# Feed-forward parts of a two-block network on one core: the fourth and fifth chunk sums in the banks of Strassen's products, the root's spread behind block 70

## The chip, the core and the metric

The kernel runs on one core of a Trainium2 chip. The metric is the device time of one execution in microseconds (us). A core has five engines that run their own instruction streams side by side: PE (TensorE: matrix products; its weight loads are listed apart as PEld), DVE (VectorE), ACT (ScalarE), POOL (GpSimd) and SP (SyncE, which issues the transfers here). PSUM is the memory into which PE accumulates; this kernel uses it as eight banks, in three pools.

## The reference, cut to what matters

Two layers over 256 tokens of width 2048. Each layer has a mixer (a convolution and pooling mixer in the first layer, a short gated convolution in the second) and a feed-forward part, each added to the residual stream `h`:

```
h = h + mixer(h)
h = h + swiglu(rms_norm(h, ffn_norm[i]), w_gate[i], w_up[i], w_down[i])
# swiglu(h, g, u, d) = (silu(h @ g) * (h @ u)) @ d,   g, u: 2048 x 5632,   d: 5632 x 2048
# rms_norm: h * rsqrt(mean(h*h over the 2048) + 1e-6) * gain
```

The root of a token's mean square is one number per token. It is not multiplied into `h`: the matrix products run on `h * gain`, and the root is multiplied into their results afterwards. So the products can begin before the root is known; only what leaves PSUM needs it.

## The kernel before, in words

**Precision.** All is single precision in and out. Each 128x128 block of weights is split into a rounded part `hi` (ACT, line 200) and the remainder `lo` (DVE, line 201), and so are the activations (`xs`: ACT line 316, DVE line 317). A block then takes three matmuls over 256 tokens, `product`, lines 290 to 292. "Block" below means those three. Weights come in tiles of 16 blocks and are split eight blocks at a time, some pieces ahead; the split pieces lie in five buffers for `hi` and five for `lo`.

**Chunk sums.** In a feed-forward part 16 blocks make one chunk sum: 128 columns of the gate or of the up matrix over the whole width. Gate and up take turns. A chunk sum lies in a PSUM bank of the pool `acc`, which has three banks, until DVE has multiplied it by the root (`scaled`, line 444). A second pool, `s`, has four banks for the second way in which a part of the columns is computed: Strassen's seven products (`s_stream`, lines 746 to 748), which begin later and need token-major sums of `h` (`s_forms`, lines 662 to 669, ACT and DVE, eight pieces). The last PSUM bank, `st`, holds small sums.

**The root.** After the last residual chunk: square (ACT, line 421), sum over chunks (POOL, line 423), sum over the partitions by PE (line 359), root on ACT (line 372), a few operations on 128x2 numbers on DVE (lines 373 to 380), a diagonal matrix (DVE, line 384), a matmul of it with ones that spreads the root over all partitions (PE, line 392), a copy to SBUF (DVE, line 430). Then the first chunk sums can be evicted. In the source all of this is called after the first chunk sum of the part, and the eight pieces of `s_forms` are queued there, one every six blocks.

**What sets the order.** A table, `KINDS`, says for each step whether a block of the column products or a step of Strassen's products comes next; `LEAD` (line 60) says how many blocks precede the first Strassen step of the first window of a feed-forward part, and runs of 14 steps are then dealt out evenly. On top of it a scheduler that simulates a timeline sets each engine's own order when the program is built, so an instruction can stand earlier or later on its engine than in the source. On the chip each engine works through its own order.

**Names.** FFN0 and FFN1 are the feed-forward parts of the two layers. Blocks are counted from 0 at the start of such a part: chunk sum 1 is blocks 0 to 15, chunk sum 4 blocks 48 to 63, chunk sum 5 blocks 64 to 79.

## Time and profile before

| | |
|---|---|
| median of 3 runs | 2024.15 us (2020.88 to 2025.91) |
| the profiled execution, its own time | 2023.4 us |
| its span, first to last instruction | 2021.4 us |
| mean granted TensorE clock | 0.994 |
| PE busy | 1991.6 us (99%) |
| DVE busy | 1693.5 us (84%) |
| ACT busy | 1145.3 us (57%) |
| POOL busy | 197.6 us (10%) |

The profile is of one execution. Its span leaves out 2.0 us around the first and the last instruction that the time holds. A busy share is a mean over stages with different limits; a stall of some microseconds shows in a stage's own rows only. In the timeline a row gives the start, the duration, the engine, the source line, the operation, its output and inputs, and in brackets how long the engine sat idle ahead of it and what ended that. Matmul rows overlap: each shows some 0.28 us, while the next begins 0.11 us after it. In the view of engine windows each stretch has, for each engine, its busy time and in brackets the count of instructions, and then the granted clock and the share of the DMA engines.

### The profile page before, as it was taken

The page shows a single profiled execution, that of the slowest core. Times are in us where ns is not written, and L with a number is a line of the kernel's source. Part 1 is how long each engine was busy: PE and PEld are TensorE (multiplying, and loading weights), DVE is VectorE, ACT ScalarE, POOL GpSimd, SP SyncE. Part 2 cuts the span into 40 slices and gives each one's busy share as a digit, 9 for nine tenths or more (in the row PEclk, how much of TensorE's full clock was granted, in tenths as well). Part 3 has the DMA queues.
Part 4 walks back from the last instruction along what each step waited for, and adds up shares of the span by engine and source line. Part 5 has one row for each costly group of instructions (what it writes and reads, how often), then busy time and mean ns, then how long its engine had stood idle before and what let it go on. Part 6 is the DMA issues. An engine that isn't in the chain of part 4 may idle for free.

```text
span 2021.4 us, 41502 instructions
## 1 busy us (share of the span) xinstructions
PE 1991.6 (99%) x17370; PEld 1987.4 (98%) x17370; DVE 1693.5 (84%) x2370; ACT 1145.3 (57%) x1492; POOL 197.6 (10%) x180
## 2 busy tenths in 40 slices
PE   9999899999999999999999999999999999999998
PEld 8999899999999999999999999999999999999998
DVE  6998878988898888998666666778888898899995
ACT  7786665555555555556444444655555555555555
POOL 2996200000000000002000001100000000000003
PEclk9999999999999999999999999999999999999999
DMA  8555345555556555555555555455555464545562
GB/s 332 187 185 191 134 150 215 200 191 206 197 200 216 201 208 190 205 195 220 194 189 190 200 195 189 167 188 208 188 196 219 171 224 180 221 177 200 209 231 83
DMA packets 56923, 396.16 MB, mean 196 GB/s; under 512 B 6432, under 2 KB 7200, under 8 KB 9760
## 3 DMA queue, kind: packets, MB, share of 16 engines
q1 hardware_dynamic: 56736, 393.52, 52.7%
q8 instruction: 136, 2.23, 0.4%
q14 instruction: 51, 0.42, 0.1%
HBM read 391.39 MB, written 2.10 MB: 195 GB/s over the span
## 4 chain that ended last, share of the span: by engine, by line
PE 92%; DVE 5%; ACT 1%; DMA 1%; issue 0%; SPq 0%; DVEq 0%; ACTq 0%
PE acc L290 23%; PE acc L291 23%; PE acc L292 23%; PE s L748 7%; PE s L746 7%; PE s L747 7%; DVE side L514 1%; DVE side L516 1%; DVE lo L201 1%; PE acc L702 0%; ACT hi L200 0%; DMA rows<-in_xtok 0%; DMA h<-in_xT 0%; ACT w L662 0%; DVE sf L669 0%
## 5 line engine op out<-in xcount | busy, mean ns | idle before, releaser
L200 ACT CAST hi<-w 128x1024 fp32r<-128x1024 f32 (+2 forms) x916 | 915.3, 1009 | 787.8 <-PE acc L291 481.1
L201 DVE TENSOR_TENSOR lo<-w,hi 128x1024 fp32r<-128x1024 f32 (+2 forms) x867 | 1004.6, 1174 | 214.4 <-ACT hi L200 199.0
L290 PE MATMUL acc<-xs,hi 128*128 128x256 f32 x2688 | 743.5, 277 | 6.8 <-DVE gate L444 3.5
L291 PE MATMUL acc<-xs,hi 128*128 128x256 f32 x2688 | 742.1, 277 | 0.0
L292 PE MATMUL acc<-xs,lo 128*128 128x256 f32 x2688 | 738.9, 277 | 0.1
L290 PEld LDWEIGHTS acc<-xs,hi 128*128 128x128 f32 x2688 | 507.7, 189 | 8.6 <-ACT hi L200 3.3
L291 PEld LDWEIGHTS acc<-xs,hi 128*128 128x128 f32 x2688 | 507.7, 189 | 0.0
L292 PEld LDWEIGHTS acc<-xs,lo 128*128 128x128 f32 x2688 | 505.4, 189 | 0.6 <-DVE lo L201 0.5
L290 PE MATMUL acc<-y,hi 128*128 128x256 f32 x1408 | 388.5, 276 | 0.0
L291 PE MATMUL acc<-y,hi 128*128 128x256 f32 x1408 | 387.6, 276 | 0.0
L292 PE MATMUL acc<-y,lo 128*128 128x256 f32 x1408 | 385.5, 276 | 0.0
L291 PEld LDWEIGHTS acc<-y,hi 128*128 128x128 f32 x1408 | 264.4, 188 | 0.0
L290 PEld LDWEIGHTS acc<-y,hi 128*128 128x128 f32 x1408 | 264.2, 188 | 0.0
L292 PEld LDWEIGHTS acc<-y,lo 128*128 128x128 f32 x1408 | 263.3, 188 | 0.0
L423 POOL TENSOR_TENSOR sumsq<-sumsq,sq 128x256 f32<-128x256 f32 x56 | 55.7, 995 | 1540.6 <-ACT sq L421 1540.4
L746 PE MATMUL s<-hi,sf 128*128 128x256 f32 x704 | 193.7, 276 | 0.0
L747 PE MATMUL s<-hi,sf 128*128 128x256 f32 x704 | 193.3, 276 | 0.0
L748 PE MATMUL s<-lo,sf 128*128 128x256 f32 x704 | 191.7, 276 | 0.0
L747 PE MATMUL s<-hi,xs 128*128 128x256 f32 x528 | 146.1, 277 | 0.0
L748 PE MATMUL s<-lo,xs 128*128 128x256 f32 x528 | 145.9, 276 | 0.0
L746 PE MATMUL s<-hi,xs 128*128 128x256 f32 x528 | 145.7, 276 | 0.0
L747 PEld LDWEIGHTS s<-hi,sf 128*128 128x128 f32 x704 | 132.2, 188 | 0.0
(162 smaller groups left out, 2386.3 us busy)
## 6 DMA issues: line engine op xcount, KB each, us to landing
w<-in_wall SPq DMA_DIRECT2D x365, 1024.0 KB, 4.9
w<-in_wall SPq DMA_DIRECT2D x7, 512.0 KB, 8.3
rows<-in_xtok SPq DMA_DIRECT2D x2, 1024.0 KB, 7.8
h<-in_xT SPq DMA_DIRECT2D x7, 256.0 KB, 7.3
out<-res SPq DMA_DIRECT2D x2, 512.0 KB, 2.7
out<-res SPq DMA_DIRECT2D x2, 384.0 KB, 2.8
v<-in_vec SPq DMA_DIRECT2D x1, 260.0 KB, 6.7
h<-in_xT SPq DMA_DIRECT2D x2, 128.0 KB, 2.4
```

The lines of the kernel that those rows point to most:

```text
L200: nc.scalar.copy(hi, src)
L201: engine.tensor_tensor(out=lo, in0=src, in1=hi, op=ALU.subtract)
L290: nc.tensor.matmul(acc, hi, x[:, :T], start=first, stop=False)
L291: nc.tensor.matmul(acc, hi, x[:, T:], start=False, stop=False)
L292: nc.tensor.matmul(acc, lo, x[:, :T], start=False, stop=last)
L423: nc.gpsimd.tensor_tensor(out=self.sums[0], in0=self.sums[0], in1=sq, op=ALU.add)
L514: nc.vector.scalar_tensor_tensor(out=dst, in0=src, scalar=wt, in1=dst, op0=ALU.mult, op1=ALU.add)
L516: nc.vector.tensor_tensor(out=side, in0=side, in1=prods.pop((c, k)), op=ALU.add)
L746: nc.tensor.matmul(acc, xh, hi, start=first, stop=False, skip_group_check=True)
L747: nc.tensor.matmul(acc, xl, hi, start=False, stop=False, skip_group_check=True)
L748: nc.tensor.matmul(acc, xh, lo, start=False, stop=last, skip_group_check=True)
```

## The change

In the first window of each feed-forward part:

- `LEAD` goes from 76 to 96. By the table the first run of Strassen's steps moves from behind 113 blocks to behind 128, and the four runs then stand 32 blocks apart in place of 37; the last one stays behind block 224.
- The fourth and fifth chunk sums go into the first two banks of the pool `s`, which Strassen's products use later.
- The work on the root is cut in two. The first part (sums, root, diagonal) is called after the first chunk sum as before. The second part (the spreading matmul and the copy) is called at 70 blocks, and the scheduler is told to put that matmul behind the last matmul issued so far. Evictions of chunk sums that end before are held back and done right then.
- The eight pieces of `s_forms` are queued from 28 blocks on in place of 16.

Nothing is computed that was not computed before, and nothing is left out.

```diff
-LEAD = (76,) + (0,) * len(SECTIONS)
+LEAD = (96,) + (0,) * len(SECTIONS)
+FORMS_AT, REST_AT = 28, 70
...
-        nc.tensor.matmul(acc, lo, x[:, :T], start=False, stop=last)
+        state_pe["last"] = nc.tensor.matmul(acc, lo, x[:, :T], start=False, stop=last).ins
...
-        return spread or over_features(diag)
+        if halves:
+            return spread
+        return partial(over_features, diag)
...
-        def rstd(self, sums=None, keep=None):
-            st = rsqrt_of(*self.sums, scale=1.0 / D, st=sums, keep=keep)
-            r = tmp.tile([P, T], F32, name="rstd", bufs=1)
-            nc.vector.tensor_copy(out=r, in_=st)
-            return r
+        def rstd(self, sums=None, keep=None, behind=False):
+            spread = rsqrt_of(*self.sums, scale=1.0 / D, st=sums, keep=keep)
+
+            def rest():
+                with tc.issue_after(state_pe["last"]) if behind else nullcontext():
+                    st = spread()
+                r = tmp.tile([P, T], F32, name="rstd", bufs=1)
+                nc.vector.tensor_copy(out=r, in_=st)
+                return r
+
+            return rest if behind else rest()
...
             def rstd():
-                state["r"] = norm.rstd(keep=rtok)
+                state["rest"] = norm.rstd(keep=rtok, behind=True)
+
+            def token_sums():
                 scratch = wst.tile([P, 16 * P], F32, name="w")
...
+                            if w == 0 and jobs in (3, 4):
+                                acc = banks["s"].tile([P, 2 * T], F32, name=f"s{jobs - 3}")[:, :T]
+                            else:
+                                acc = new_acc()
...
+                                at = cursor["P"] - first_block
+                                if w == 0 and at == FORMS_AT:
+                                    token_sums()
+                                if w == 0 and at == REST_AT:
+                                    state["r"] = state["rest"]()
+                                    while held:
+                                        held.pop(0)()
+                            jobs += 1
+                            if w == 0 and jobs == 1:
+                                rstd()
+                            evict = partial(up_of, pair, c, acc) if half else partial(gate_of, pair, acc)
+                            if "r" in state:
+                                evict()
                             else:
+                                held.append(evict)
```

Line numbers shift in the changed kernel: there 291 to 293 are the three matmuls of a block, 202 is `lo`, 361 the sum over partitions, 386 the diagonal, 396 the spreading matmul, 438 the copy, 454 the multiplication by the root.

**First place: PE around the spread in FFN0.** `acc_3547` is the third chunk sum, `acc_3633` the fourth, `s1_3685` the fifth in the changed kernel; the numbers are tiles. Before:

```order
L290 MATMUL acc_3547<-xs_75,hi_3468 128x256
L291 MATMUL acc_3547<-xs_75,hi_3468 128x256
L292 MATMUL acc_3547<-xs_75,lo_3469 128x256
L392 MATMUL st_3459<-diag_3456,ones_76 128x256
L290 MATMUL acc_3633<-xs_75,hi_3504 128x256
L291 MATMUL acc_3633<-xs_75,hi_3504 128x256
L292 MATMUL acc_3633<-xs_75,lo_3505 128x256
```

The change:

```order
L292 MATMUL s0_3602<-xs_75,hi_3520 128x256
L293 MATMUL s0_3602<-xs_75,lo_3521 128x256
L291 MATMUL s1_3685<-xs_75,hi_3564 128x256
...
L293 MATMUL s1_3685<-xs_75,lo_3565 128x256
L396 MATMUL st_3716<-diag_3456,ones_76 128x256
L291 MATMUL s1_3685<-xs_75,hi_3564 128x256
```

Before, the spread stands between block 47 and block 48; in the change it stands behind block 69, inside the fifth chunk sum. In FFN1 it stands at the same places.

**Second place: DVE around the copy of the root in FFN0.** `lo_...` are split weights for blocks 72 and 80 (before) and 80, 88, 96 and 104 (change), `sf` are the last pieces of `s_forms`. Before:

```order
L201 TENSOR_TENSOR lo_3635<-w_3508,hi_3634 128x1024
L669 TENSOR_TENSOR sf_3384<-w_3463,sf_3384 128x512
L380 COPY rtok_3385<-st_3441 128x2
L384 TENSOR_TENSOR diag_3456<-v_73,st_3441 128x128 x2
L201 TENSOR_TENSOR lo_3671<-w_3596,hi_3670 128x1024
L430 COPY rstd_3461<-st_3459 128x256
L444 TENSOR_TENSOR gate_3464<-acc_3386,rstd_3461 128x256
L444 TENSOR_TENSOR val_3542<-acc_3467,rstd_3461 128x256
L444 TENSOR_TENSOR gate_3630<-acc_3547,rstd_3461 128x256
```

The change:

```order
L386 TENSOR_TENSOR diag_3456<-v_73,st_3441 128x128 x2
...
L202 TENSOR_TENSOR lo_3640<-w_3568,hi_3639 128x1024
L679 TENSOR_TENSOR sf_3384<-w_3506,sf_3384 128x512
L202 TENSOR_TENSOR lo_3687<-w_3568,hi_3686 128x1024
L679 TENSOR_TENSOR sf_3384<-w_3506,sf_3384 128x512
L202 TENSOR_TENSOR lo_3743<-w_3643,hi_3742 128x1024
L438 COPY rstd_3718<-st_3716 128x256
L454 TENSOR_TENSOR gate_3720<-acc_3386,rstd_3718 128x256
L454 TENSOR_TENSOR val_3723<-acc_3459,rstd_3718 128x256
L454 TENSOR_TENSOR gate_3728<-acc_3519,rstd_3718 128x256
L454 TENSOR_TENSOR val_3731<-s0_3602,rstd_3718 128x256
L202 TENSOR_TENSOR lo_3785<-w_3643,hi_3784 128x1024
```

Between the diagonal and the copy there are now the last pieces of `s_forms` and three splits, where one split stood before; behind the copy four multiplications by the root follow at once.

**Third place: PE at the border of the first mixer and FFN0.** `acc_3336` is the mixer's last sum, `acc_3386` the first chunk sum, `sumsq` the sum of squares over the chunks but the last. Before:

```order
L291 MATMUL acc_3336<-cat_195,hi_3193 128x256
L292 MATMUL acc_3336<-cat_195,lo_3194 128x256
L290 MATMUL acc_3386<-xs_75,hi_3228 128x256
...
L290 MATMUL acc_3386<-xs_75,hi_3265 128x256
L359 MATMUL st_3441<-ones_76,sumsq_2830 128x1 x2
L359 MATMUL st_3441<-ones_76,sq_3368 128x1 x2
```

The change:

```order
L292 MATMUL acc_3336<-cat_195,hi_3193 128x256
L293 MATMUL acc_3336<-cat_195,lo_3194 128x256
L361 MATMUL st_3441<-ones_76,sumsq_2830 128x1 x2
L291 MATMUL acc_3386<-xs_75,hi_3228 128x256
```

The first two of the four small matmuls that sum the squares stood at the end of the first chunk sum and now stand ahead of the first block; the other two stand some three blocks into the second chunk sum. In FFN1 the first two stay behind 15 blocks. On DVE the first piece of `s_forms` stands behind the mixer's last addition to `h` in the change, and ahead of the last but one before.

More of the change, by code (lines that the diff above doesn't have):

```diff
@@ L308, in block_kernel @@
     phase = [None]
+    state_pe = {}
     def split(dst, src, scale=None):
@@ L588, in ln_rstd @@
             st = state["st"]
-            state["rstd"] = spread_over(st, st[:, :2], 1.0)
+            state["rstd"] = spread_over(st, st[:, :2], 1.0)()
         def ln_out(c):
@@ L678, in swiglu @@
             state = {}
+            first_block = cursor["P"]
             def rstd():
-                state["r"] = norm.rstd(keep=rtok)
+                state["rest"] = norm.rstd(keep=rtok, behind=True)
+            def token_sums():
                 scratch = wst.tile([P, 16 * P], F32, name="w")
@@ L755, in p_stream, with gate_of, up_of @@
                     base = SLOT_A * (w % 2)
-                    for c in range(2 * g, 2 * g + p):
-                        accs = []
-                        for _ in range(2):
-                            acc = new_acc()
+                    jobs, held = 0, []
+                    def gate_of(pair, acc):
+                        gate = scaled(acc, state["r"], "gate")
+                        nc.scalar.activation(gate, gate, AF.Silu)
+                        pair.append(gate)
+                    def up_of(pair, c, acc):
+                        up = scaled(acc, state["r"], "val")
+                        nc.vector.tensor_tensor(out=up, in0=up, in1=pair[0], op=ALU.mult)
+                        split(y[:, base + c, :], up)
+                    for c in range(2 * g, 2 * g + p):
+                        pair = []
+                        for half in range(2):
+                            if w == 0 and jobs in (3, 4):
+                                acc = banks["s"].tile([P, 2 * T], F32, name=f"s{jobs - 3}")[:, :T]
+                            else:
+                                acc = new_acc()
                             for k in every:
@@ L762, in p_stream @@
                                 product(acc, *next_block(), norm.xs[:, k, :], k == 0, k == NC - 1)
-                            if len(accs):
-                                up = scaled(acc, state["r"], "val")
-                                gate = accs[0]
-                                nc.vector.tensor_tensor(out=up, in0=up, in1=gate, op=ALU.mult)
-                                split(y[:, base + c, :], up)
-                            else:
-                                if "r" not in state:
-                                    rstd()
-                                gate = scaled(acc, state["r"], "gate")
-                                nc.scalar.activation(gate, gate, AF.Silu)
-                                accs.append(gate)
+                                at = cursor["P"] - first_block
[11 more added lines that the diff above has]
+                                evict()
+                            else:
+                                held.append(evict)
                 if w:
```

## The prediction

> **What bounds the kernel now.** I read the page first: busy shares, then the chain that ended last.
>
> ```profile
> PE 1991.6 (99%) x17370; PEld 1987.4 (98%) x17370; DVE 1693.5 (84%) x2370; ACT 1145.3 (57%) x1492; POOL 197.6 (10%) x180
> PE 92%; DVE 5%; ACT 1%; DMA 1%; issue 0%; SPq 0%; DVEq 0%; ACTq 0%
> ```
>
> PE is busy nearly throughout and the chain runs over it, so only PE time counts: fewer or shorter matmuls, or fewer gaps. The change adds and removes no matmul. So I looked for gaps by PE's own waits. In the start of FFN0 (253 to 300 us) two of them stand side by side:
>
> ```profile
> PE st L392 <- DVE diag L384: 1.9, 1, 1.9
> PE acc L290 <- DVE gate L444: 1.3, 1, 1.3
> ```
>
> The same two lines stand in the start of FFN1. The engine windows show what goes on there; the second and third rows are the two stretches of FFN0, and the last two those of FFN1.
>
> ```profile
> 254.00:271.30 17.30, 17.30 (x152) 17.26 (x152) 17.09 (x42) 15.48 (x27) 1.75 (x1) 1.00 0.49 171
> 271.30:275.20 3.90, 0.83 (x4) 0.30 (x2) 3.87 (x9) 2.40 (x3) 0.00 (x0) 1.00 0.61 210
> 275.20:279.60 4.40, 4.36 (x24) 4.39 (x25) 1.32 (x4) 1.09 (x3) 0.00 (x0) 0.61 0.80 339
> 340.00:900.00 560.00, 560.00 (x4920) 560.00 (x4919) 504.10 (x655) 312.21 (x366) 0.00 (x0) 1.00 0.54 201
> 1323.50:1326.90 3.40, 0.83 (x4) 0.30 (x3) 3.37 (x9) 2.41 (x3) 0.00 (x0) 1.00 0.64 181
> 1326.90:1330.90 4.00, 3.97 (x21) 4.00 (x22) 1.30 (x4) 1.07 (x3) 0.00 (x0) 0.57 0.88 371
> ```
>
> Between 340 and 900 us PE runs 4920 instructions in 560 us without a gap, so that stage gives nothing. In 3.9 us from 271.3 on PE runs almost nothing, and in the 4.4 us behind it its granted clock is 0.61. The timeline of PE has the gap itself:
>
> ```profile
> 271.18 0.28 PE L292 MATMUL acc<-xs,lo 128*128 128x256 f32 x1
> 273.31 0.67 PE L392 MATMUL st<-diag,ones 128*128 128x256 f32 x2 [1.85 <-DVE diag L384]
> 275.24 0.36 PE L290 MATMUL acc<-xs,hi 128*128 128x256 f32 x1 [1.26 <-DVE gate L444]
> ...
> 281.67 0.28 PE L292 MATMUL acc<-xs,lo 128*128 128x256 f32 x1
> ```
>
> The third chunk sum (block 47) ends, the spread of the root waits for the diagonal, block 48 waits for the first multiplication by the root, which frees a bank. Three accumulator banks were full. The row that ends the excerpt is the last matmul of block 61.
>
> To price it I need the pace. Windows of the third matmul of a block alone (line 292); each count has one more, whose tail reaches into the window:
>
> ```profile
> 262.40:271.25 8.85, 7.16 (x27) 4.89 (x27) 1.00 0.65 214
> 271.25:281.75 10.50, 4.60 (x15) 3.45 (x15) 0.84 0.57 222
> 1323.45:1332.70 9.25, 4.03 (x13) 3.05 (x13) 0.82 0.62 229
> ```
>
> Row one: 26 blocks from 262.34 to 271.18, 0.340 us per block. Row two: 14 blocks (48 to 61) end 10.49 us after block 47 (271.18 to 281.67); at pace they take 4.76. **FFN0 loses 5.73 us.** Row three: 12 blocks take 9.23 us (1323.39 to 1332.62) in place of 4.08. **FFN1 loses 5.15 us.** Together 10.88 us, 0.54% of the time. In FFN0 4.0 us of it are standing still (271.29 to 275.24) and 1.8 the slow clock behind it, in FFN1 3.4 and 1.7.
>
> **The change part by part.** *The spread behind block 69, chunk sums 4 and 5 in other banks.* PE then has work for blocks 48 to 79 without an eviction, so both gaps go if three things are in time: the diagonal, the copy of the root with the first multiplication, and the split weights.
>
> What the spread costs where it need not wait is shown by the second layer's mixer, where the same two instructions stand amid a chunk sum (PE, then DVE):
>
> ```profile
> 968.63 0.28 PE L291 MATMUL acc<-xs,hi 128*128 128x256 f32 x1
> 968.74 0.59 PE L392 MATMUL st<-diag,ones 128*128 128x256 f32 x2
> 968.99 0.47 PE L292 MATMUL acc<-xs,lo 128*128 128x256 f32 x1
> 969.29 0.28 PE L290 MATMUL acc<-xs,hi 128*128 128x256 f32 x1
> ```
> ```profile
> 969.37 0.42 DVE L430 COPY rstd<-st 128x256 f32<-128x256 f32 x1 [1.18 <-PE st L392]
> ```
>
> From 968.63 to 969.29 there are 0.66 us where two matmuls at pace take 0.23: the spread costs 0.43 us. It stays in each part: 2 x 0.43 = 0.86 us of the 10.88 are not won. The copy begins 0.63 us after the spread.
>
> *Is DVE in time?* DVE is the engine that was late, with 17.09 busy us of 17.30 ahead of the gap:
>
> ```profile
> 253.37 0.42 DVE L437 TENSOR_TENSOR h<-acc,h 128x256 f32<-128x256 f32 x1
> ...
> 269.08 1.22 DVE L201 TENSOR_TENSOR lo<-w,hi 128x1024 fp32r<-128x1024 f32 x1
> 270.22 0.68 DVE L669 TENSOR_TENSOR sf<-w,sf 128x512 fp32r<-128x512 f32 x1
> ...
> 272.69 0.47 DVE L384 TENSOR_TENSOR diag<-v,st 128x128 f32<-128x128 f32 x2
> ...
> 274.22 0.42 DVE L430 COPY rstd<-st 128x256 f32<-128x256 f32 x1
> ```
>
> From the last addition to `h` to the copy are 20.85 us. In the changed order there stand between these two one split more (269.08 to 270.22: 1.14 us), twelve more 128x128 operations of `s_forms`, which stood ahead of that addition before, and one `xs` less:
>
> ```profile
> 245.50 0.41 DVE L437 TENSOR_TENSOR h<-acc,h 128x256 f32<-128x256 f32 x1
> 248.22 0.41 DVE L437 TENSOR_TENSOR h<-acc,h 128x256 f32<-128x256 f32 x1
> 249.40 0.28 DVE L664 TENSOR_TENSOR w<-w 128x128 f32<-128x128 f32 x1
> 249.60 0.28 DVE L667 TENSOR_TENSOR w<-w 128x128 f32<-128x128 f32 x1
> ```
>
> Such an operation takes 0.20 us (249.40 to 249.60), so 20.85 + 1.14 + 2.40 - 0.4 = 24.0 us. The additions come every 2.72 us (245.50, 248.22), so undisturbed the last one falls two periods on, at 253.66, and DVE reaches the copy at 277.7. PE comes to the spread at block 70: 271.29 + 22 x 0.340 = 278.8; the copy begins at 279.4. So DVE waits for PE, not PE for DVE, with 1.7 us to spare; the diagonal is done at least 3.4 us earlier, since three splits stand between it and the copy. In FFN1:
>
> ```profile
> 1306.58 0.41 DVE L437 TENSOR_TENSOR h<-acc,h 128x256 f32<-128x256 f32 x1
> 1325.92 0.41 DVE L430 COPY rstd<-st 128x256 f32<-128x256 f32 x1
> ```
>
> 19.34 + 1.14 + 2.60 (thirteen operations) = 23.1 us, counted from 1306.5: 1329.6. The spread is due at 1323.50 + 7.48 = 1331.0, the copy at 1331.6; 2.0 us to spare.
>
> *Is the first bank free for block 80?* Before, 1.02 us pass from the copy's start to PE's next block (274.22 to 275.24). So the bank is free at 279.4 + 1.0 = 280.4; block 80 is due at 278.8 + 0.43 + 3.40 = 282.6. The next two banks follow at 0.34 us each and are wanted 16 blocks later. In FFN1: 1332.6 against 1334.8. The spare time is 2.2 us in both.
>
> *What waits behind the copy.* On DVE the splits of blocks 104 and on, on ACT the load of the activation table for the gate and the next `hi`. These are wanted at 282.6 + 24 x 0.34 = 290.8 or later, some ten us after the copy. The rows that price them:
>
> ```profile
> 272.44 1.28 ACT L772 ACT_TABLE_LOAD   x1
> ```
> ```profile
> L200 ACT CAST hi<-w 128x1024 fp32r<-128x1024 f32 (+2 forms) x916 | 915.3, 1009 | 787.8 <-PE acc L291 481.1
> L201 DVE TENSOR_TENSOR lo<-w,hi 128x1024 fp32r<-128x1024 f32 (+2 forms) x867 | 1004.6, 1174 | 214.4 <-ACT hi L200 199.0
> ```
>
> A table load of 1.28 us and a piece of 1.0 us on ACT and 1.2 on DVE fit in there. And what `hi` waits for most is PE (481.1 of 787.8 us): the splits run ahead as far as the buffers allow. So I put nothing down for them.
>
> *Squares ahead of block 0 in FFN0.* The first two small matmuls now stand ahead of the first block and want the sum of squares:
>
> ```profile
> 247.01 1.00 POOL L423 TENSOR_TENSOR sumsq<-sumsq,sq 128x256 f32<-128x256 f32 x1 [1.72 <-ACT sq L421]
> 254.22 1.75 POOL L423 TENSOR_TENSOR sumsq<-sumsq,sq 128x256 f32<-128x256 f32 x1 [0.35 <-ACT sq L421]
> ```
>
> ```profile
> 253.06 0.28 PE L292 MATMUL acc<-cat,lo 128*128 128x256 f32 x1
> 253.94 0.35 PE L290 MATMUL acc<-xs,hi 128*128 128x256 f32 x1 [0.61 <-DVE h L437]
> ```
>
> Before, that sum ended at 255.97, which would hold PE 2.0 us from 253.94. But it was late, since the pieces of `s_forms` stood ahead of the last additions on ACT and DVE. By the period of 2.72 us the last addition of squares falls at 247.01 + 2 x 2.72 = 252.45 and ends at 253.45 (its usual 1.00 us). PE has a gap there anyway, since block 0 waits for the last addition to `h`. That one is due at 253.66 in place of 253.37, so block 0 begins 0.28 us later. Bounds: 0.4 us won (the two small matmuls fall into the gap) to 2.0 us lost. I take 0.28 lost, since the steady rows are nearer to the changed order than the disturbed ones.
>
> *Strassen's steps later, `s_forms` later.* The number of steps is the same. The runs stand 32 blocks apart, against 26 in the windows from 340 to 900 us, where PE has no gap. First step at about 299 us, last piece of `s_forms` near 277. Nothing.
>
> *The sum.* 10.88 - 0.86 - 0.28 = 9.74 us won. Ends: 10.88 + 0.4 = 11.3 (spread and sums for nothing) and 10.88 - 0.86 - 2.0 = 8.0. The profiled execution took 2023.4 us, so 2013.7; it lies 0.75 under the median of the runs, so a median of **2014.4 us**, 0.48% less. Its own range, with the runs' spread of about 2.5 us, is 2011 to 2018.
>
> **The rivals.** 0.3% (6.1 us) is about what a measurement of this kernel can tell from no change.
>
> *A. The stall moves to block 80.* If DVE or ACT reach the copy over 2.2 us later than I count, PE stands at block 80 as it did at block 48. For it: DVE has no slack ahead of the copy (17.09 of 17.30 us), and three splits stand ahead of it that need buffers which PE frees. Against it: the split nearest to the copy, for block 96, needs the buffer of blocks 56 to 63, free at 276.7; with 1.0 us on ACT and 1.2 on DVE it is done at 278.9, still ahead of 279.4. If one of the parts stalls again at the old price: 2023.4 - 9.74 + 5.4 = 2019.1, on the median's scale 2019.8. That is within 0.3%.
>
> *B. The early squares hold PE.* If POOL ends as before, at 255.97, block 0 of FFN0 begins 2.0 us late, which is 1.7 us more than I count, and 1.8 more if the clock then drops as behind the gap above: 2015.4 to 2017.2, on the median's scale 2016.1 to 2018.0. Still faster.
>
> [...]
>
> *C. Nothing is won.* That the stall is hidden by something later, so that a gap that closes opens elsewhere by as much: 2023.4, median 2024.2. Against it: behind the gap PE runs for 600 us and more without one, so a block that begins earlier ends everything earlier, if weights arrive, and with the DMA engines at 0.49 to 0.88 of their time in the stretches above they do.
>
> *D. Slower: Strassen's runs starve.* In the first window a run comes every 46 steps now, 51 before. A run's four split pieces displace those of the blocks behind it; if each of the eight runs of both parts made PE wait for one piece (1.0 us on ACT and 1.2 on DVE, 2.2 together): 17.6 - 9.7 = 7.9 us slower, 2031.3, on the median's scale 2032. It decides from the first row on that shows PE waiting for `lo` behind a run. Against it: 26 blocks between runs do without such a wait from 340 to 900 us.
>
> **How the numbers follow.** Forecast 0.77; A 0.09; B 0.06; C 0.04; D 0.04. Faster by over 0.3%: nearly all of the forecast's and of B's share, 0.81. Within 0.3%: A and C and what noise takes from the forecast, 0.14. Slower: D, and a share of noise, 0.05. The range of 8 in 10 takes in the forecast's own and B's and ends just short of A's middle: 2011 to 2019.4 us.
>
> **What would show it.** In the changed profile PE should have, besides the wait of block 0 itself, no row of over 0.5 us idle between 254 and 300 us nor between 1306 and 1345; the granted clock there should be 1.00; the spread should stand amid fifth-chunk matmuls at about 278.8 with 0.4 us around it; the copy of the root should be listed as waiting for PE. Line 292's counterpart should end block 61 near 276.2 in place of 281.67. A wait of PE for a multiplication by the root at block 80 shows A, one for POOL or ACT ahead of block 0 shows B, waits for `hi` or `lo` from 299 us on show D. The forecast is wrong if the gaps are gone and the span is still over 2016.

## The result, and the profile after

| | before | changed |
|---|---|---|
| median (6 runs each) | 2024.45 us | 2014.17 us (2012.95 to 2015.66) |
| the profiled execution, its own time | 2023.40 us | 2013.79 us |
| its span | 2021.4 us | 2011.4 us |
| mean granted clock | 0.994 | 0.996 |

The ratio is 0.9955, with an interval of 0.9944 to 0.9965: faster by 0.35 to 0.56%. The addition to `h` is line 447 in the changed kernel.

The page of the changed kernel, busy times:

```profile
PE 1985.7 (99%) x17370; PEld 1982.2 (99%) x17370; DVE 1691.9 (84%) x2370; ACT 1144.1 (57%) x1492; POOL 196.9 (10%) x180
```

PE does the same 17370 instructions and DVE the same 2370. In the waits of PE one row of 0.2 us is left in FFN0's start (253 to 300 us; the small matmuls ahead of block 0, whose row stands further down), and none in FFN1's (1305 to 1345 us). The windows of the engines, at the places where the two gaps were (the same columns as before):

```profile
271.30:275.20 3.90, 3.90 (x37) 3.90 (x36) 3.90 (x10) 2.75 (x4) 0.00 (x0) 1.00 0.57 155
275.20:279.60 4.40, 4.40 (x40) 4.35 (x39) 3.65 (x5) 1.56 (x2) 0.00 (x0) 1.00 0.72 255
1323.50:1326.90 3.40, 3.40 (x30) 3.35 (x30) 2.20 (x4) 1.06 (x1) 0.00 (x0) 1.00 0.69 248
1326.90:1330.90 4.00, 4.00 (x37) 4.00 (x36) 3.53 (x8) 3.96 (x6) 0.00 (x0) 1.00 0.77 291
```

PE runs 37 and 40 instructions where it ran 4 and 24, at a granted clock of 1.00. The timeline of PE and DVE around the spread in FFN0 (PE's rows first):

```profile
271.22 0.28 PE L293 MATMUL acc<-xs,lo 128*128 128x256 f32 x1
...
275.98 0.28 PE L293 MATMUL s<-xs,lo 128*128 128x256 f32 x1
...
278.70 0.28 PE L293 MATMUL s<-xs,lo 128*128 128x256 f32 x1
278.81 0.59 PE L396 MATMUL st<-diag,ones 128*128 128x256 f32 x2
...
279.48 0.28 PE L293 MATMUL s<-xs,lo 128*128 128x256 f32 x1
```
```profile
272.51 0.47 DVE L386 TENSOR_TENSOR diag<-v,st 128x128 f32<-128x128 f32 x2
...
277.94 1.23 DVE L202 TENSOR_TENSOR lo<-w,hi 128x1024 fp32r<-128x1024 f32 x1 [0.48 <-ACT hi L201]
279.44 0.42 DVE L438 COPY rstd<-st 128x256 f32<-128x256 f32 x1 [0.28 <-PE st L396]
279.90 0.42 DVE L454 TENSOR_TENSOR gate<-acc,rstd 128x256 f32<-128x256 f32 x1
```

The first two rows are the third matmuls of block 47 and of block 61: 4.76 us for 14 blocks, exactly the pace, in place of 10.49. The spread stands between two blocks of the fifth chunk sum; the third matmuls around it lie 0.78 us apart (278.70 to 279.48) where 0.34 is the pace, so it costs 0.44 us. The diagonal is done at 272.98. The last split ahead of the copy waits 0.48 us for `hi` and ends at 279.17, so the copy at 279.44 waits for PE, but only 0.28 us.

Where the time went can be told more sharply than by medians. I cut each trace at two matmuls that every variant has: the last one of the first mixer and the last one of the second (here the rows of the changed kernel, then that of before, whose 253.06 the prediction shows).

```profile
253.28 0.28 PE L293 MATMUL acc<-cat,lo 128*128 128x256 f32 x1
...
1300.85 0.28 PE L293 MATMUL acc<-z,lo 128*128 128x256 f32 x1
```
```profile
1306.13 0.28 PE L292 MATMUL acc<-z,lo 128*128 128x256 f32 x1
```

| part of the trace, us | before | changed | won |
|---|---|---|---|
| FFN0 and the second mixer | 1053.07 | 1047.57 | 5.50 |
| FFN1 to the end of the span | 715.27 | 710.55 | 4.72 |
| both | 1768.34 | 1758.12 | 10.22 |

The first mixer itself took 0.22 us more in this execution (253.28 against 253.06). That part varies by some microseconds between executions, while the sum of the other two repeats within 0.2 us for kernels that should be equal there (below: 1768.34, 1768.49, 1768.40). So the experiments are read by this sum, and their medians are given beside it. One of the seven executions of the kernel with the spread ahead of block 80 took 11339.83 us, for a cause that stays open, and the median given below is that of the other six (2018.24 with it).

### The profile page after: what moved, and what is told of

It reads as the page before. It is cut to its first block, busy times and chain, and to the rows that moved or that the text cites. A ratio compares the mean times of both kernels' runs of the same rounds, so it can differ in the third digit from the quotient of the medians.

```text
span 2011.4 us, 41493 instructions
## 1 busy us (share of the span) xinstructions
PE 1985.7 (99%) x17370; PEld 1982.2 (99%) x17370; DVE 1691.9 (84%) x2370; ACT 1144.1 (57%) x1492; POOL 196.9 (10%) x180
## 4 chain that ended last, share of the span: by engine, by line
PE 93%; DVE 4%; DMA 1%; ACT 1%; issue 0%; SPq 0%; DVEq 0%; POOL 0%; ACTq 0%; POOLq 0%
PE acc L291 24%; PE acc L292 23%; PE acc L293 23%; PE s L761 7%; PE s L759 7%; PE s L760 7%; DVE side L524 1%; DVE side L526 1%; DVE lo L202 1%; PE acc L715 0%; DMA rows<-in_xtok 0%; PE s L293 0%; PE s L291 0%; PE s L292 0%; DMA h<-in_xT 0%
## 5 line engine op out<-in xcount | busy, mean ns | idle before, releaser
L291 PE MATMUL acc<-xs,hi 128*128 128x256 f32 x2624 | 723.0, 276 | 5.5 <-ACT hi L201 4.4
L292 PE MATMUL acc<-xs,hi 128*128 128x256 f32 x2624 | 722.2, 276 | 0.0
L293 PE MATMUL acc<-xs,lo 128*128 128x256 f32 x2624 | 719.1, 276 | 0.1
L291 PEld LDWEIGHTS acc<-xs,hi 128*128 128x128 f32 x2624 | 493.3, 188 | 6.4 <-ACT hi L201 5.0
L292 PEld LDWEIGHTS acc<-xs,hi 128*128 128x128 f32 x2624 | 493.4, 188 | 0.0
L293 PEld LDWEIGHTS acc<-xs,lo 128*128 128x128 f32 x2624 | 491.1, 188 | 0.6 <-DVE lo L202 0.5
```

Source lines behind the costliest of these rows:

```text
L291: nc.tensor.matmul(acc, hi, x[:, :T], start=first, stop=False)
L292: nc.tensor.matmul(acc, hi, x[:, T:], start=False, stop=False)
L293: state_pe["last"] = nc.tensor.matmul(acc, lo, x[:, :T], start=False, stop=last).ins
```

## The experiments

| kernel | FFN0 and second mixer | FFN1 to end | sum | median, ratio to before (interval) |
|---|---|---|---|---|
| before | 1053.07 | 715.27 | 1768.34 | |
| changed | 1047.57 | 710.55 | 1758.12 | 2014.17, 0.9955 (0.9944 to 0.9965) |
| later products alone | 1053.01 | 715.48 | 1768.49 | 2023.63, 0.9997 (0.9987 to 1.0006) |
| changed, products early | 1047.59 | 710.57 | 1758.16 | 2014.14, 0.9950 (0.9935 to 0.9964) |
| new code, old order | 1053.02 | 715.38 | 1768.40 | 2024.73, 1.0003 (0.9994 to 1.0013) |
| the same, PE kept busy | 1051.40 | 713.87 | 1765.27 | 2019.68, 0.9979 (0.9969 to 0.9989) |
| spread ahead of block 80 | 1048.89 | 711.96 | 1760.85 | 2017.80, 0.9974 (0.9962 to 0.9986) |
| one bank, spread behind 58 | 1048.88 | 711.30 | 1760.18 | 2014.38, 0.9955 (0.9940 to 0.9970) |
| two banks, spread behind 58 | 1047.57 | 710.55 | 1758.12 | 2011.54, 0.9943 (0.9930 to 0.9957) |
| the same once more | 1047.59 | 710.59 | 1758.18 | 2013.79, 0.9960 (0.9946 to 0.9973) |
| `s_forms` from block 16 | 1047.75 | 710.82 | 1758.57 | 2014.09, 0.9954 (0.9938 to 0.9969) |
| no bank, forms behind the copy | 1049.29 | 711.55 | 1760.84 | 2015.91, 0.9965 (0.9951 to 0.9979) |
| changed, first mixer's spread earlier | 1047.59 | 710.57 | 1758.16 | 2014.23, 0.9954 (0.9941 to 0.9966) |
| the same, `s_forms` from 16, banks swapped | 1047.75 | 710.57 | 1758.32 | 2012.93, 0.9948 (0.9934 to 0.9962) |

**Strassen's products later: does it pay?** The edit alone on the kernel before, and the change without it.

```diff
-LEAD = (76,) + (0,) * len(SECTIONS)
+LEAD = (96,) + (0,) * len(SECTIONS)
```

> The kernel before with one edit of the change alone: Strassen's products begin 20 blocks later in each feed-forward part; the spread of the root stays behind the third chunk sum. My theory (the time comes from two gaps at that spread and nothing else) expects both gaps unchanged: PE idle for 1.9 and 1.3 us in FFN0's start, third matmul of the 14 blocks 48 to 61 over 10.5 us, and a time within 1 us of the kernel before (2024.4). Rival 1 (the later products themselves gain, by leaving DVE and the transfers freer) expects 2 to 4 us less, 2020 to 2022. Rival 2 (denser products starve PE) expects more than 2026 and waits of PE for lo behind 299 us.

> The change without its later begin of Strassen's products: these begin at block 113 of a feed-forward part as before the fifth sum's bank is long free. My theory expects the same as the changed kernel, 2014.2 within 1 us, span near 2011.4, no idle row of PE over 0.5 us behind block 0: the products' place pays nothing here and its edit only has to keep them out of banks in use. Rival (the earlier begin piles products' split pieces onto the first window behind the copy of the root, when DVE is still behind): waits of PE for hi or lo between 283 and 310 us, 1 to 4 us slower than the changed kernel.

Measured: alone 1768.49 in place of 1768.34; left out 1758.16 in place of 1758.12. The gaps of the first kernel are the old ones (waits of PE of 1.9 us for the diagonal and 1.3 for the first multiplication in FFN0, of 1.3 and 1.3 in FFN1), and no kernel of the two waits for `hi` or `lo` behind 299 us. So the later begin is worth nothing either way. With the products at block 113 the two borrowed banks have long been read: in the changed kernel the last multiplication by the root out of them starts at 283.57, when PE is near block 82.

**Is it the change of the code? What is the slow clock worth?** The changed code with the old order as a control, and the same with matmuls into a free bank where PE would stand (16 ahead of the spread, 9 behind it; their results are used by nobody).

```diff
-LEAD = (96,) + (0,) * len(SECTIONS)
-FORMS_AT, REST_AT = 28, 70
+LEAD = (76,) + (0,) * len(SECTIONS)
+FORMS_AT, REST_AT = 16, 48
...
-                            if w == 0 and jobs in (3, 4):
+                            if w == 0 and jobs in ():
```
and in the second kernel also
```diff
+                                    state_pe["last"] = fill(16, state_pe["last"])
                                     state["r"] = state["rest"]()
+                                    fill(9, state_pe["spread"])
```

> The changed kernel's code with the order of the kernel before: no chunk sum in another bank, spread right behind block 47, squares at block 16, products begin as before. A control for the other runs. My theory expects the time of the kernel before, 2024.4 within 1 us, with the gap at block 48 of 3.9 us in FFN0 and a granted clock near 0.6 in the 4.4 us behind it. Rival (the rewriting of the code gains something of its own): less than 2022.

> The control with extra work: 16 matmuls of 128x128 by 128x256 into a free bank ahead of the spread of the root and 9 behind it, in each feed-forward part, so that PE computes (what nobody uses) where it would stand idle. The stall for the diagonal and the copy stays, about 3.9 and 3.4 us. My theory splits the loss of a part in standing time (4.0 and 3.4 us) and a slow clock behind it (1.8 and 1.7 us), so it expects a granted clock of 1.00 in the 4.4 us behind the gap and 3.5 us less than the control, less what the filler overshoots (at most 0.5 us per part): 2021 to 2022, the profiled span 2.5 to 3.5 us below the control's. Rival (the clock drops for another reason than PE's idleness, say the spread's two-pass f32 matmul or a throttle on power): the clock is near 0.6 again and the time no better than the control's 2024.4.

The control is the kernel before (1768.40). Its gap in FFN0, by the third matmuls of blocks 47 and 48 and of two behind them, and the engine window behind the gap:

```profile
271.91 0.28 PE L293 MATMUL acc<-xs,lo 128*128 128x256 f32 x1
...
276.30 0.28 PE L293 MATMUL acc<-xs,lo 128*128 128x256 f32 x1
...
277.26 0.41 PE L293 MATMUL acc<-xs,lo 128*128 128x256 f32 x1
277.90 0.41 PE L293 MATMUL acc<-xs,lo 128*128 128x256 f32 x1
```
```profile
275.80:280.20 4.40, 4.22 (x23) 4.25 (x24) 1.45 (x5) 1.16 (x3) 0.00 (x0) 0.61 0.83 350
```

And with the filler (line 800):

```profile
273.45 0.28 PE L293 MATMUL acc<-xs,lo 128*128 128x256 f32 x1
273.56 2.05 PE L800 MATMUL s<-xs 128*128 128x256 f32 x16
...
275.90 1.41 PE L800 MATMUL s<-xs 128*128 128x256 f32 x9
...
277.82 0.28 PE L293 MATMUL acc<-xs,lo 128*128 128x256 f32 x1
...
278.18 0.28 PE L293 MATMUL acc<-xs,lo 128*128 128x256 f32 x1
```
```profile
275.70:280.00 4.30, 4.10 (x32) 3.87 (x33) 3.05 (x7) 1.45 (x4) 0.00 (x0) 1.00 0.92 381
```

From block 47 to block 48 the two kernels take the same, 4.39 us (271.91 to 276.30) and 4.37 (273.45 to 277.82): the stall is untouched. Behind it blocks follow every 0.64 us in the one (277.26 to 277.90) and every 0.36 in the other (277.82 to 278.18), at a clock of 0.61 and 1.00. The filler wins 1.62 us in FFN0 and 1.51 in FFN1, 3.13 in all. In FFN1 it was too long: from block 47 to block 48 that kernel takes 3.99 us (1323.99 to 1327.98) in place of 3.86 (1324.08 to 1327.94), so the clock is worth 1.64 there. So 3.26 of the 10.88 us of the stalls were the clock behind them. With matmuls in PE's idle time the slow clock is gone (1.00 in place of 0.61), though the spread stands in both kernels. The 3.5 us I expected for the clock were 0.24 too many. The medians lie 5 us apart, more than the traces show behind the first mixer, and that of 2019.68 is below the 2021 to 2022 expected. The profiled spans lie 1.6 us apart, less than the 2.5 to 3.5 expected; the first mixer, which ended at 255.33 us in place of 253.80, makes up for that. The interval of the second against the kernel before (0.21%, from 0.11 to 0.31%) holds 3.1.

**Must the spread stand ahead of the last free block?**

```diff
-FORMS_AT, REST_AT = 28, 70
+FORMS_AT, REST_AT = 28, 80
```

> The changed kernel with the spread of the root put right ahead of block 80, where no bank is free any more, in place of behind block 69. My theory: nothing covers the copy and the first multiplication, so PE stands for about 0.63 us (spread to copy) plus 1.0 us (copy to next block) less the spread's own 0.43 counted already: 1.2 to 1.7 us per part, with the clock at 1.00, since that is far shorter than the gap before: 2.4 to 3.4 us more than the changed kernel, 2016.6 to 2017.6. The diagonal is then long ready. Rival 1 (the gap brings the slow clock with it as before): 1.7 us more per part, 2020 or above. Rival 2 (it is the splits, not the banks, that count): no difference, 2014.2.

Measured 1760.85, 2.73 us more than the changed kernel (1.32 and 1.41). PE in FFN0:

```profile
285.29 0.59 PE L396 MATMUL st<-diag,ones 128*128 128x256 f32 x2
...
286.95 0.36 PE L291 MATMUL acc<-xs,hi 128*128 128x256 f32 x1 [1.07 <-DVE gate L454]
```

The copy begins 0.63 us after the spread and the multiplication 0.46 us after that, and block 80 waits 1.07 us for the bank. The median of 2017.80 is a little above the range expected; in the profiled execution (2019.47) the first mixer ended at 256.35 us, three later than in the changed kernel's, so that part of it is not of this edit. Behind this wait matmuls follow every 0.11 us (eleven steps from 287.15 to 288.40), which is the pace at a granted clock of 1.00.

**How many banks?** The fourth chunk sum alone in another bank, the spread behind block 58; then both banks with the spread at that same place, twice. In the second edit the spread is called at block 48, and the scheduler sets it behind block 58 of FFN0 all the same; in FFN1 it stands behind block 59 in each of these kernels.

```diff
-FORMS_AT, REST_AT = 28, 70
+FORMS_AT, REST_AT = 28, 58
...
-                            if w == 0 and jobs in (3, 4):
+                            if w == 0 and jobs == 3:
```
and
```diff
-FORMS_AT, REST_AT = 28, 70
+FORMS_AT, REST_AT = 28, 48
```

> The changed kernel with one chunk sum in another bank in place of two (the fourth alone), the spread in the middle of that fourth sum (behind block 58). PE then has 5 blocks (1.7 us) behind the spread and 16 blocks (5.4 us) in all from block 48 on. My theory: the diagonal was ready 1.9 us after block 47 before the change and the copy could begin 24.0 us after the last addition to h (277.7 us in FFN0); the spread of FFN0 is due at 274.9, block 64 at 277.2; so PE waits at block 64 until about 278.7 at worst (277.7 + 1.0), 0.5 to 1.5 us in FFN0 and 0 to 1 us in FFN1, without the slow clock: 0.5 to 2.5 us more than the changed kernel, 2014.7 to 2016.7. Rival (both banks are needed): a stall of 2 us or more and the slow clock behind it in a part, 2018 or above.

> The changed kernel with the spread of the root in the middle of the fourth chunk sum (behind block 58, as in the run with one bank) and both banks kept. Measured from the last addition to h of the first mixer to the end, the changed kernel took 1757.5 us and the run with one bank 1759.6. My theory (what counts is that PE has blocks to compute until the first bank is free; the place of the spread only has to be behind the diagonal) expects no wait of PE and the changed kernel's 1757.5 within 0.5 us, median 2014.2 within 1.5. Rival (the early spread itself costs, since PE comes to it before the diagonal or the copy then displaces splits that block 64 and on need): a wait of PE of 1 us or more in a part, 1758.5 to 1760.

> The kernel with both banks and the spread behind block 58 once more, unchanged. Its trace is the changed kernel's from the last addition to h on (1757.5 us), and its first mixer, in which no instruction stands elsewhere, ended 2.3 us earlier (251.57 against 253.87 us), which made its median 2011.5 in place of 2014.2. Theory 1 (the first mixer's length varies by itself from execution to execution, and four runs happened to be short): a median nearer to 2014, between 2012.5 and 2015. Theory 2 (something fixed in this build makes its first mixer shorter): 2011 to 2012 again, last addition to h near 251.6, and no wait of PE for the total of the layer norm in it.

The expectations of the later runs count from the last addition to `h`, a little behind my cut; by it the changed kernel has 1757.5 (253.87 to the end at 2011.4).

With one bank: 1760.18, 2.06 us more, as expected. The median of 2014.38 is below the range expected; in the profiled execution the first mixer ended at 251.62, 1.7 us earlier than in the changed kernel's. Rows of PE and DVE in FFN0:

```profile
273.53 0.59 PE L396 MATMUL st<-diag,ones 128*128 128x256 f32 x2
...
276.75 0.35 PE L291 MATMUL acc<-xs,hi 128*128 128x256 f32 x1 [1.02 <-ACT hi L201]
```
```profile
275.72 0.42 DVE L438 COPY rstd<-st 128x256 f32<-128x256 f32 x1
276.18 0.42 DVE L454 TENSOR_TENSOR gate<-acc,rstd 128x256 f32<-128x256 f32 x1
```
```profile
275.65 1.04 ACT L201 CAST hi<-w 128x1024 fp32r<-128x1024 f32 x1 [1.59 <-PE s L292]
```

The wait is put down to `hi`; the multiplication that frees the bank ended at 276.60 and that cast at 276.69, so both were late. The copy begins 1.6 us after the spread is through, because DVE comes to it only then. With two banks at the same spread PE waits for no bank in FFN0 or FFN1, 1758.12 and 1758.18, and the copy may come when DVE comes:

```profile
275.08 0.41 DVE L438 COPY rstd<-st 128x256 f32<-128x256 f32 x1
```

The spread's place does not matter as long as PE has blocks until DVE has got to the copy. Here DVE gets there 24.10 us behind the last matmul of the first mixer (250.98), which in the changed kernel's time is 277.38. But this order has two splits between the diagonal and the copy, where the changed kernel has three, so it does not show when DVE is ready there.

The same kernel had a median of 2011.54 and then, on another chip, of 2013.79, with equal traces behind the first mixer. So theory 1 holds: its apparent lead over the changed kernel was the first mixer's variation.

**`s_forms` queued from block 16, as before the change.** The expectations call this the squares; what the edit moves are the pieces of `s_forms`, and the small matmuls of the squares come to stand elsewhere by it.

```diff
-FORMS_AT, REST_AT = 28, 70
+FORMS_AT, REST_AT = 16, 70
```

> The changed kernel with the token sums and the squares' forms at block 16 of the part as before the change, in place of block 28; spread and banks as in the change. My theory: DVE has the same number of instructions ahead of the copy or a few more (forms ahead of the last additions to h), the copy still waits for PE and not for DVE, so the time is that of the changed kernel, 2014.2 within 1 us; FFN0's block 0 may begin up to 0.3 us earlier or up to 2.0 us later by the pieces that stand ahead of the last addition. Rival (the forms' later place is what took the load off DVE ahead of the diagonal): the copy comes more than 2.2 us later than in the changed kernel, PE waits at block 80, 1 to 5 us slower.

Measured 1758.57, 0.45 us more (0.18 and 0.27); the copy still waits for PE, so the forms' place took no load off DVE that counted. In FFN0 both groups of small matmuls stand inside the chunk sums again, as before the change. The 0.27 us of FFN1 are not in PE's work: its last group of matmuls begins 701.21 us behind the cut (1299.78 to 2000.99), in the changed kernel 701.19 (1300.85 to 2002.04). They lie behind it, in the end of the kernel, which was longer in this execution; why stays open.

**Was a bank needed at all?** No bank; the spread inside the third chunk sum; the forms on DVE behind the copy.

```diff
-FORMS_AT, REST_AT = 28, 70
+FORMS_AT, REST_AT = 41, 40
...
+            def forms_behind(*what):
+                with tc.issue_after(state_pe["copy"]):
+                    s_forms(*what)
...
-                            if w == 0 and jobs in (3, 4):
+                            if w == 0 and jobs in ():
```

> No chunk sum in another bank at all; the spread stands inside the third chunk sum (behind block 40) and the squares' forms on DVE stand behind the copy of the root, so that the twelve and more pieces of 0.2 us and the 128x512 ones are out of the diagonal's way. It tells whether a bank was needed, or only an earlier diagonal. Theory 1 (the diagonal is late by what stands ahead of it on DVE): it is ready 4 us or more earlier, and PE reads a free bank at block 48: both gaps gone but for at most 0.5 us each, 2014 to 2016. Theory 2 (DVE is full with splits anyway, which the next blocks need; moving the forms only lets more splits go ahead): the diagonal is not early enough, a gap of 1 us or more stays at the spread or at block 48 in each part, 2017 to 2022.

Measured 1760.84: 7.50 of the 10.22 us are won without a bank, 1.72 and 1.00 are left. DVE, then PE, in FFN0:

```profile
253.16 0.41 DVE L447 TENSOR_TENSOR h<-acc,h 128x256 f32<-128x256 f32 x1
...
268.47 0.47 DVE L386 TENSOR_TENSOR diag<-v,st 128x128 f32<-128x128 f32 x2
...
271.26 0.89 DVE L674 TENSOR_TENSOR w<-w 128x128 f32<-128x128 f32 x4
272.07 0.42 DVE L454 TENSOR_TENSOR gate<-acc,rstd 128x256 f32<-128x256 f32 x1
```
```profile
272.63 0.36 PE L291 MATMUL acc<-xs,hi 128*128 128x256 f32 x1 [1.39 <-DVE gate L454]
```

The diagonal begins 15.3 us after the last addition to `h` (253.16), in the changed kernel 18.6 (253.87 to 272.51) and before 19.3 (253.37 to 272.69). So it was late by what stood ahead of it on DVE, as theory 1 said. But block 48 still waits 1.39 us, more than theory 1 allowed. Of this 0.81 us are four pieces of the forms (271.26 to 272.07) that were put between the copy and the multiplication that frees the bank. The spread also stands behind block 46, and not behind block 40 as expected, so that one block alone covers the copy. In FFN1 it stands behind block 41; there the same four pieces take 0.80 us and block 48 waits 0.69. Both theories missed the size. No slow clock shows in it: FFN0's part loses 1.72 us, 0.33 more than the wait, where the slow clock was worth 1.62.

**A version beyond the change.** The same remedy in the first mixer; then with `s_forms` from block 16 and the two groups of banks swapped.

```diff
-                product(acc, hi, lo, xs[:, k, :], first, last)
+                with tc.issue_after(state_pe["spread"]) if i == spread_at else nullcontext():
+                    product(acc, hi, lo, xs[:, k, :], first, last)
...
-                (acc,) = matmul_chunks(xs, every)
+                (acc,) = matmul_chunks(xs, every, spread_at=7 if g == M0_ORDER[0][1] and j == 0 else None)
```
and
```diff
-FORMS_AT, REST_AT = 28, 70
+FORMS_AT, REST_AT = 16, 70
...
-    banks["acc"] = ctx.enter_context(tc.tile_pool(name="ps", bufs=3, space=PSUM))
     banks["s"] = ctx.enter_context(tc.tile_pool(name="ps_s", bufs=1, space=PSUM))
+    banks["acc"] = ctx.enter_context(tc.tile_pool(name="ps", bufs=3, space=PSUM))
```

> The changed kernel and, beside it, the same remedy in the first mixer: there PE waits 0.95 us for the first multiplication by the root at 40.56 us, 1.2 us behind the spread at 38.9, though the diagonal was ready at 34.8. The spread is put behind the seventh block of the chunk sum ahead of it, so that the copy and the multiplication lie beside seven blocks or more. Theory: the wait at 40.56 goes; 0.7 to 1.2 us less ahead of the last addition to h, nothing changed behind it (1757.5), median 2013.0 to 2013.5, which the start's own variation of 2 us may hide. Rival (the start is bound by the arrival of the weights, with the DMA engines busy 0.95 of 20 to 45 us): PE waits for hi a little later by as much, nothing gained.

> As the run before it, and the squares at block 16 again, and the two groups of accumulator banks swapped in place, so that block 0 of FFN0 does not get the bank that the last addition to h reads. Until now PE stands for 0.6 us ahead of block 0 of FFN0 (for that addition, or for the two small matmuls of the squares that fill the gap). With squares at block 16 alone the time from the last addition to the end was 1758.3. Theory: block 0 follows the last matmul of the mixer at once, 0.6 to 0.9 us less than that: 1757.4 to 1757.7, that is no better than the changed kernel there by more than 0.2 us, since the small matmuls cost 0.5 us at block 16; together with the first mixer's spread a median of 2012.8 to 2013.5. Rival (block 0 waits for its first input xs or for hi and not for the bank): 1758.3 as with the squares at block 16 alone.

In the first, the wait at 40 us is gone, and another has grown: four of PE's waits up to 253 us in the changed kernel, then the same in this one.

```profile
PE acc L291 <- ACT cat L607: 3.4, 1, 3.4
PE st L396 <- DVE diag L386: 2.8, 1, 2.8
PE acc L291 <- DVE xs L319: 2.4, 1, 2.4
PE st L553 <- DVE total L538: 1.0, 1, 1.0
```
```profile
PE acc L291 <- ACT cat L608: 3.6, 1, 3.6
PE st L554 <- DVE total L539: 3.0, 1, 3.0
PE acc L291 <- DVE xs L320: 2.2, 1, 2.2
PE st L397 <- DVE diag L387: 1.4, 1, 1.4
```

The wait of 0.9 us for the multiplication by the root, which the changed kernel has at 40.56 us, has no row any more. PE waits 3.0 us for `total`, DVE's running sum of the layer norm, in place of 1.0, and 1.4 for the diagonal in place of 2.8. The four add up to 9.6 and 10.2 us, so 0.6 of the 0.9 us won early are given back there; the mixer ended at 254.24 us, which is inside its variation. Neither theory had this: the time goes back at waits for DVE and not for weights. The edit also moved instructions of DVE, ACT and POOL behind it, so which of them is the bound there stays open.

In the second, block 0 of FFN0 still waits 0.61 us for the addition to `h`, and FFN0's part is that of `s_forms` from block 16 alone (1047.75 both). So, if the swap gave block 0 another bank as meant, it was not the bank; what it needs of that addition stays open. The 0.25 us by which FFN1 is shorter than with `s_forms` from block 16 alone lie behind PE's last matmuls again (701.21 us behind the cut in both). Neither version beats the changed kernel by anything that the parts or the medians can tell.

## Why the prediction was right

It said 2014.4 us within 2011.0 to 2019.4 and faster at 0.81; the median is 2014.17. Its steps:

- *The two stalls are worth 10.88 us and go.* Right: 14 blocks at the pace, 4.76 us, in FFN0; no wait and clock 1.00 in FFN1. Their division was a little off: the slow clock is 1.62 and 1.64 us by the run with the filler, where I had 1.8 and 1.7.
- *The spread costs 0.43 us in each part.* 0.44 measured.
- *DVE is in time for the copy, with 1.7 us to spare in FFN0 and 2.0 in FFN1.* In time, but by 0.28 us in each (the idle time ahead of the copy at 279.44 and at 1326.33). The spread stood at 278.81 where I had 278.8, but DVE was done with what stands ahead of the copy at 279.17 and not at 277.7: 25.3 us behind the addition to `h` (253.87), where the sum had 24.0. For 1.5 us of these DVE stood idle and waited for ACT (the root 0.40 us, `hi` 0.61 and 0.48), and the sum counted its work alone. Rival A's working, which had the last split done at 278.9, was nearer. It cost nothing, since the copy only has to come in time for block 80. The diagonal was ready 5.8 us before its spread.
- *The first bank is free at 280.4, block 80 due at 282.6.* The multiplication that frees it ran from 279.90 to 280.32, and PE passed block 80 without a wait.
- *Table load, splits, later products: nothing.* Right; the two runs on the products show the last.
- *Block 0 of FFN0 begins 0.28 us later, counted as a loss.* The step that failed, if only in size: the term is 0.18 us won (below).
- *The sum.* By measured terms 5.73 - 0.44 + 0.18 = 5.47 in FFN0 and 5.15 - 0.45 = 4.70 in FFN1, against 5.50 and 4.72 in the parts. I had 9.74 in all; 10.22 were won, 0.22 lost in the first mixer's variation, and 0.4 more of the time lie outside the span (2.4 us in place of 2.0). So the profiled execution came out at 2013.79 us against 2013.7 by luck: these two took back what the parts won beyond the forecast. With a first mixer that moves by some microseconds, the 0.2 us between the median and its forecast are luck as well.

The term of block 0. The start itself came as forecast: 1.15 us behind the mixer's last matmul (253.28) in place of 0.88 before (253.06 to 253.94). PE of the changed kernel:

```profile
253.72 0.60 PE L361 MATMUL st<-ones,sumsq 128*128 128x1 f32 x4 [0.17 <-POOL sumsq L427]
254.43 0.36 PE L291 MATMUL acc<-xs,hi 128*128 128x256 f32 x1
```

But the small matmuls that now fill this gap no longer stand inside a chunk sum. Before, both groups stood there:

```profile
259.05 0.28 PE L292 MATMUL acc<-xs,lo 128*128 128x256 f32 x1
...
259.28 0.50 PE L359 MATMUL st<-ones,sumsq 128*128 128x1 f32 x4
...
260.41 0.28 PE L292 MATMUL acc<-xs,lo 128*128 128x256 f32 x1
```

Four matmuls from 259.05 to 260.41 (three of them, and the second group of small ones, are left out) take 1.36 us in place of 0.45 at pace, so the two groups cost 0.91; now one of them is left. From block 0 to the end of block 47 the changed kernel takes 16.79 us (254.43 to 271.22) in place of 17.24 (253.94 to 271.18), 0.45 less. So the term is 0.45 - 0.27 = 0.18 us won and not 0.28 lost, inside its bounds (0.4 won to 2.0 lost); the bound that I passed over named the reason. The run with `s_forms` from block 16 bears it out: with both groups inside the chunk sums again, FFN0 takes 0.18 us more.

The rivals. *A*: no stall at block 80. Its price of 5.4 us was that of the old stall, 3.9 and 3.4 us long with a clock of 0.61 and 0.57 behind it; with the spread right ahead of block 80 a part lost 1.32 and 1.41 us, and behind the wait of 1.07 us in FFN0 the matmuls kept their pace of 0.11 us. *B*: the sum of squares held PE for 0.17 us, not 2.0. Which of its two prices would have held, with the slow clock or without, stays open: behind a wait of 2.32 to 2.38 us the clock fell in five traces and stayed at 1.00 in six (last section). *C*: nothing opened elsewhere; both parts keep what they won. *D*: no wait for `hi` or `lo` behind 299 us, with the products at either place.

## What to carry to other kernels

A short stall of PE behind a late scalar chain was removed here by giving PE blocks that need no eviction, as many as the chain needs to get through the engine that is full; where in those blocks the chain's own matmul stood was of no account (behind block 58 or 69 of FFN0, 1758.12 us both), as long as enough of them followed it to cover the copy and the first multiplication. Moving other work out of the chain's way on the full engine, without a bank, won 7.50 of the 10.22 us. When you ask whether an engine is in time, count what it waits for, and not its work alone. Count a stall with the slow clock behind it (here 3.3 of 10.9 us), and look at what was hidden in the gap that closes or opens. For changes below half a per cent compare parts of traces between instructions that both kernels have: here they repeat within 0.2 us, while the medians move by two with a part that was not touched.

## What the hardware showed that I had not expected

The first mixer varies: its last matmul came between 250.98 and 256.35 us in fourteen traces, though all but the last two variants run the same instructions in the same order up to its last six microseconds. A part of that is the arrival of the first weights (up to 253 us PE waits for `hi` for 2.7 us in all in the kernel before, 4.4 in the changed one and 5.6 in the one with the banks swapped; in the changed kernel the `hi` at 7.13 us itself waits 1.47 us for the transfer of its weights). Another is the clock. The changed kernel and the one with `s_forms` from block 16 have the same wait there, and not the same clock behind it (timeline of PE, and the window behind, of each):

```profile
153.50 0.58 PE L291 MATMUL acc<-cat,hi 128*128 128x256 f32 x1 [2.35 <-DVE xs L319]
```
```profile
154.00:159.00 5.00, 5.00 (x34) 5.00 (x34) 4.86 (x11) 4.05 (x9) 4.92 (x4) 0.73 0.56 210
```
```profile
153.40 0.38 PE L291 MATMUL acc<-cat,hi 128*128 128x256 f32 x1 [2.32 <-DVE xs L319]
```
```profile
154.00:159.00 5.00, 5.00 (x47) 5.00 (x46) 4.86 (x11) 4.05 (x9) 4.92 (x4) 1.00 0.61 211
```

After 2.35 us of waiting one ran at a granted clock of 0.73 for 5 us, 34 matmuls, the other, after 2.32 us, at 1.00, 47 matmuls: 1.5 us at 0.113 each. In eleven of the fourteen traces this wait is 2.32 to 2.38 us long; behind it the clock fell in five of them (0.68 to 0.82 from 154 to 159 us) and stayed at 1.00 in six.

Behind the waits of 1.02 to 1.39 us in the experiments on FFN0 I found no slow clock: the part lost 0.25 to 0.33 us more than the wait, where the slow clock was worth 1.62. Behind the old gaps the clock was 0.61 and 0.57 in the kernel before and 0.61 in FFN0 of the control. The length of a wait alone does not tell: a wait of 3.18 us that ends at 24.90 us in the changed kernel left the clock at 1.00 (21.50 to 28.40 us). What else counts none of these runs shows.
